# The expert layer's input moved to the bottom of the partitions, and the loads of scattered gates begun within the first layer

## The chip, the core and the metric

The kernel runs on one core of one Trainium2 chip. The metric is device time in microseconds (us) of one execution; lower is better. TensorE is called PE here, its weight loads PEld, VectorE DVE, ScalarE ACT, GpSimd POOL, and SyncE SP. SP does no arithmetic here: it issues most DMA transfers, one after the other, and an issue that waits holds back those behind it.

## The reference

A batch of 256 tokens of width 1024 goes through two transformer blocks in float32. The first block mixes by sliding-window attention and retention, with gated output, and has a SwiGLU layer. The second block mixes by spatial gating and banded attention with a learned bias over relative positions, and has a PEER expert layer, in which this change lies:

```python
def block(xb):                                   # 128 tokens at a time
    q = (xb @ w_query).reshape(128, 8, 2, 128)   # 8 heads, two half queries
    sc = jnp.einsum('thpd,hpkd->thpk', q, sub_keys)
    s_top, i_top = lax.top_k(sc, 16)
    ...                                          # 16 x 16 candidates of each head
    best, pos = lax.top_k(cand, 16)
    eidx = jnp.take_along_axis(cand_idx, pos, axis=-1)      # of 16384 experts
    g = jax.nn.softmax(best, axis=-1)
    u = jnp.take(expert_u, eidx, axis=0)
    h = jax.nn.gelu(jnp.einsum('thkd,td->thk', u, xb))
    vv = jnp.take(expert_v, eidx, axis=0)
    return jnp.einsum('thk,thkd->td', g * h, vv)
```

## The kernel before

**The expert layer is done densely.** Instead of gathering 128 experts for each token, the kernel computes all 16384 for all 256 tokens. The first layer (`first_layer(j)`, 128 steps) multiplies 128 experts' rows of `peer_u` with the input `xb` and puts the gelu into `S`, a tile of [128 experts, 128 steps j, 256 tokens] that holds every activation. The second layer (`second_layer`, 128 steps) multiplies `S[:, j]` with `peer_v`. In between, each entry of `S` is multiplied by its gate, which is zero for experts that were not chosen. All products are made of three matmuls with operands split in a high and a low part: `unit` (lines 77 to 100) loads a weight piece `raw` on SP's queue, ACT copies it to `whi` (line 95), and DVE makes `wlo` (line 96). There are four `raw` buffers and, in this layer, three pairs of `whi` and `wlo`. A step of the first layer is 24 matmuls of 256 columns into a bank named `mm`; a step of the second is 12 of 512 columns, into four banks `ax` that all 128 steps add to. Its left operands are the high and low part of `S[:, j]`, made by `split` (ACT line 154, DVE line 155), in tiles named `keys` (two buffers) and `q` (three).

**The gates come on two ways.** For tokens 0 to 127 (`TH` is 128) they are formed on the core: `form` and `combine` build them by matmuls of one-hot tiles during the first layer (PE line 940, names `A` and `G`) and multiply `S` by them; the tiles of this lie in a pool `comb`. `done` counts the tokens that are through. For tokens 128 to 255, POOL scatters the gates into a matrix `cmat` in HBM with indirect transfers that add (line 830). `gates(j)` (lines 1040 to 1047) loads four steps' worth, a tile `C` of [128, 4, 128], on POOL's queue and multiplies it into `S[:, j:j+4, 128:]` on DVE (line 1047).

**Memory sets the order.** SBUF pools are stacked from both ends of each partition. The pool `gates` that holds three `C` buffers takes the place of `comb`, so the kernel closes `comb` after the first layer's 128 steps and only then opens `gates`:

```python
        while done < TH:
            combine(128)
        groups.close()
        with tc.using_default_side("right"):
            gp = self.pool("gates", 1, groups)
```

The framework turns this into waits: whoever writes into a reused place waits for the last user of what lay there. `comb` also holds `gt`, the tile through which every pair of first-layer steps passes to the gates already in `S` (ACT line 1001, DVE line 1002), up to the last pair. The pool `xb` (the layer's input, 16 KB of each partition) lies on the right side too. Instructions are ordered on each engine by a scheduler that gives weight pieces a lead (`AHEAD`); `issue_after` ties a gate multiply to a place behind the latest `wlo`.

**Earlier users that the change touches.** In the first block, `aq`, `ak` and `avt` are queries, keys and values of the windowed attention, and `att` is its output. In the second block `rel` is the bias (1 MB in HBM), loaded by `load_const` (line 215) and partly overwritten by a POOL memset (line 543). `x3`, the residual input, is loaded at step 120 of the second layer into the place of `gates` (line 1077) and added to the result at the end (line 1083).

Of the kernel before, what the change touches and what calls it, by code (L numbers as in the profile page):

```python
# [7 lines left out]
F32 = mybir.dt.float32  # L8
F32R = mybir.dt.float32r
# [19 lines left out]
T = 256  # L29
TH = 128  # L30
# [13 lines left out]
class Net:  # L44
# [173 lines left out]
    def run(self):  # L218
        self.wpools, self.turn = [], 0
        with self.tc.using_default_side("right"):  # L220
            self.weights("wb", self.stack, 4, 3)
        with ExitStack() as st:
            self.res = self.pool("res", 2, st)
            self.work = self.pool("work", 2, st)
            actp = self.pool("actp", 2, st)
            with ExitStack() as sw:
                with self.tc.using_default_side("right"):
                    self.weights("wa", sw, 0, 3)
                x2, h, acc, acg = self.block1(actp)
                x3, h, acc = self.block2(actp, x2, h, acc, acg)  # L230
            self.wpools.pop()
            self.peer(st, x3, h, acc)

    def block1(self, actp):
        nc, a, tc = self.nc, self.a, self.tc
        mult, add, sub = OP.mult, OP.add, OP.subtract
        with ExitStack():
# [16 lines left out]
            both = self.const.tile([128, 192], F16, name="iota16")  # L254
# [4 lines left out]
            with ExitStack() as s1:  # L259
                p = self.pool("mix", 1, s1)  # L260
                p2 = self.pool("mix2", 2, s1)
                aq = p.tile([128, 4, T], F32, name="aq")
                ak = p.tile([128, T], F32, name="ak")
                avt = p.tile([128, T], F32, name="avt")
                av = p.tile([128, 2, 128], F32, name="av")
                rq = p.tile([128, 4, T], F32, name="rq")
                rk = p.tile([128, 4, T], F32, name="rk")
# [32 lines left out]
                                                self.ident)  # L300
                        nc.scalar.activation(av.rearrange("p a b -> p (a b)"), ps[:, :T], AF.Copy)

                att = self.new_acts(p, 4, "att", 1)
                probs = [self.att1_probs(p, tb, aq, ak, mask) for tb in range(2)]
                rv = p.tile([128, 2, D], F32, name="rv")
                room = p.tile([128, 8, 512], F32, tag="gate", name="room")
# [58 lines left out]
            with ExitStack() as s1:  # L365
                p = self.pool("ffn", 1, s1)
# [8 lines left out]
                for f in range(KF):  # L375
# [12 lines left out]
                    if 5 <= f < 21:  # L388
                        self.blanked.append(nc.sync.dma_start(out=blank[:, (f - 5) * 1024:(f - 4) * 1024],
                                                              in_=zero).ins)  # L390
                    if f == 1:
                        continue
                    for f0, (g, u) in enumerate(early, f + 1 - len(early)):
                        gu = p2.tile([128, 2, T], F32, name="gu")
                        if f0:
                            nc.vector.tensor_tensor(out=gu, in0=g, in1=R[:, None, :].to_broadcast([128, 2, T]),
                                                    op=mult)
# [129 lines left out]
    def block2(self, actp, x2, h, acc, acg):  # L527
        nc, a = self.nc, self.a
        mult, add, sub = OP.mult, OP.add, OP.subtract
        with ExitStack() as s1:  # L530
            p = self.pool("m2", 1, s1)
# [7 lines left out]
            r = self.tiny.tile([128, 2], F32, name="rd", bufs=1)  # L539
            self.rsqrt(r, ss, 2, 1.0 / D)  # L540
            nc.vector.tensor_tensor(out=r, in0=r, in1=r1, op=mult)
            bias = self.load_const(p, "rel", [128, 8, T])
            nc.gpsimd.memset(bias[0:64, :, 192:256], NEG)
            wsT = self.load_const(p, "wsT", [128, 8, 128])
            nc.gpsimd.memset(wsT[64:128, :, 0:64], 0.0)
# [169 lines left out]
    def peer(self, st, x3, h, acc):  # L715
        nc, a, tc = self.nc, self.a, self.tc
        mult, add, sub = OP.mult, OP.add, OP.subtract
        with tc.using_default_side("right"):
            xb = self.new_acts(self.pool("xb", 1), tag="xb", bufs=1)
            gs = self.pool("gs", 1).tile([128, 4, TH], F16, name="gs")  # L720
            qp = self.pool("query", 1)
            hold = self.pool("hold", 1)
            late = ExitStack()
            p = self.pool("topk", 1, late)
            pick = p.tile([128, 3, 128], F32, name="pick")
        hand = self.pool("hand", 2, st)
        x3t = tc.dram_tile([2, 128, D], F32, name="x3t")
        stop = p.tile([128, 4, 2, 2, 16], F32, name="stop")
# [31 lines left out]
        put_by = list(self.blanked)  # L760
        after = mybir.DependencyInfo(mybir.DependencyClass.Sync, mybir.DependencyReason.DATA)
# [135 lines left out]
        done = 0  # L897
        S, cp, ga = None, None, None

# [29 lines left out]
        def combine(jd):  # L929
            nonlocal done  # L930
            if made < TH:
                form()
            if len(formed) < 2 and made < TH:
                return
            t0 = done
            A, G = formed.pop(0)
            C = self.ax_bank()
            for t in range(4):
                for i in range(2):
                    nc.tensor.matmul(C[:, t * 128:t * 128 + 128], lhsT=A[:, t], rhs=G[i][:, t], start=i == 0,  # L940
                                     stop=i == 1)
            C = C.rearrange("p (t j) -> p j t", t=4)
            nc.vector.scalar_tensor_tensor(S[:, :jd, t0:t0 + 4], C[:, :jd], 1.0 / GSCALE, S[:, :jd, t0:t0 + 4],
                                           op0=mult, op1=mult)
            if jd < 128:
                nc.scalar.activation(S[:, jd:, t0:t0 + 4], C[:, jd:], AF.Copy, scale=1.0 / GSCALE)
            done += 4
# [41 lines left out]
        def first_layer(j):  # L989
            nonlocal pair  # L990
            e = j % 2
            if e == 0:
                pair = self.mm_bank()
            self.gemm_t(pair[:, e * T:e * T + T], a["peer_u"][j], xb, 8)
            if e == 0:
                return
            js = slice(j - 1, j + 1)
            p3 = pair.rearrange("p (e t) -> p e t", e=2)
            if done:
                gt = cp.tile([128, 2, TH], F32, name="gt", bufs=2)  # L1000
                nc.scalar.activation(gt[:, :, :done], p3[:, :, :done], AF.Gelu_apprx_tanh)
                nc.vector.tensor_tensor(out=S[:, js, :done], in0=S[:, js, :done], in1=gt[:, :, :done], op=mult)
            if done < T:
                nc.scalar.activation(S[:, js, done:], p3[:, :, done:], AF.Gelu_apprx_tanh)

# [2 lines left out]
            ready = pump(PQ)  # L1008
        st.close()
        S = self.pool("S", 1).tile([128, 128, T], F32, name="S")  # L1010
        c = RAWQ
        groups = ExitStack()
        for j in range(128):
            first_layer(j)
            if c < 16 and j % QE == QE - 1:
                query(c)
                c += 1
                pump(PQ)
            elif c == 16 and last:
                score(*last)  # L1020
                last = None
            if not ready:
                ready = pump(PU)
                if ready:
                    start = j
                    with tc.using_default_side("right"):
                        cp = self.pool("comb", 1, groups)
                    ga = cp.tile([128, TH], F32, name="ga")
                    nc.scalar.activation(ga, gs[:, 0], AF.Copy)
            elif j % 2:  # L1030
                while done < TH and (done + len(formed) * 4) * (GP - start) < TH * (j - start):
                    combine(j + 1)
        while done < TH:
            combine(128)
        groups.close()
        with tc.using_default_side("right"):
            gp = self.pool("gates", 1, groups)
        cview = self.cmat.rearrange("(a b t) o -> a b (t o)", a=128, b=128)

        def gates(j):  # L1040

            C = gp.tile([128, 4, 128], F32, name="C", bufs=3)
            i = nc.gpsimd.dma_start(out=C, in_=cview[:, j:j + 4]).ins
            for o in put_by:
                tc.add_manual_dep(i, o.name, after, reason="all heads have been added")
            with tc.issue_after(self.last_low):
                nc.vector.tensor_tensor(out=S[:, j:j + 4, TH:], in0=S[:, j:j + 4, TH:], in1=C, op=mult)

        gates(0)
        gates(4)  # L1050
        banks = [[self.ax_bank() for _ in range(2)] for _ in range(2)]

        def second_layer(j, tb, w, s, dhs):
# [8 lines left out]
        for j in range(128):  # L1062
            w = self.unit(a["peer_v"][j], 1024)
            s = [qp.tile([128, T], F32R, tag=t, name=t, bufs=n) for t, n in (("keys", 2), ("q", 3))]
            self.split(S[:, j], s[0], s[1])
            if j < 126:
                for tb in range(2):
                    second_layer(j, tb, w, s, ((0, 1),))
            else:
                held.append((j, w, s))  # L1070
            if j % 4 == 0 and j < 120:
                gates(j + 8)
            if j == 120:
                groups.close()
                with tc.using_default_side("right"):
                    x3 = self.pool("x3", 1).tile([128, 2, D], F32, name="x3")
                nc.sync.dma_start(out=x3, in_=x3t.rearrange("b t d -> t b d"))
# [94 lines left out]
```

## Time and profile before

| what | us |
|---|---|
| median of 3 runs (lowest, highest) | 1307.9 (1306.65, 1308.27) |
| the profiled execution: its time | 1307.3 |
| its span, first to last instruction | 1305.5 |
| PE busy with matmuls | 1285.2 (98%) |
| DVE busy | 906.7 (69%) |
| ACT busy | 719.9 (55%) |
| POOL busy | 262.9 (20%) |

The time of an execution is 1.8 us more than the span: what lies before the first and after the last instruction. PE's busy time counts the matmuls with their pipelined ends, so 98% does not say that it ran at its peak; the 20 us that are missing are waits. Times within the span are given from its start. The first layer of the experts runs from about 546 to 942 us, the second from 950 to 1301 us.

### The profile page before, as it was taken

Reading aid. Unit: us, or ns where it says so; the run is one execution under the profiler, and the core shown is the slowest. Engines: PE = TensorE matmul, PEld = TensorE weight load, DVE = VectorE, ACT = ScalarE, POOL = GpSimd, SP = SyncE. Lnnn points to the kernel's source line nnn. Section 1 sums busy time; section 2 is a strip of 40 time slices with the busy share of each in tenths; the row PEclk is TensorE's granted clock in tenths of the full one; section 3 lists DMA queues with packets and bytes.
Section 4 is the critical chain, followed back from the end, with each engine's and each line's share of the span. In section 5 each row is a group of like instructions: output and inputs, shape, how many; then the busy total and the mean of one; then the engine's idle time right before and its main releaser. Section 6 shows DMA issues by size and latency. Waiting matters only on the chain.

```text
span 1305.5 us, 23587 instructions
## 1 busy us (share of the span) xinstructions
PE 1285.2 (98%) x9125; PEld 1196.0 (92%) x9125; DVE 906.7 (69%) x1790; ACT 719.9 (55%) x1163; POOL 262.9 (20%) x173
## 2 busy tenths in 40 slices
PE   8999999999999999999999999999889999999998
PEld 7878999999999899999999999999878888888887
DVE  7767677766666877998885656665456666666665
ACT  5455545545454776554556666665445555555553
POOL 2000000000000000057778777740000000000000
PEclk9999999999999999999999999999989999999999
DMA  7645559966667535577777777765567777777764
GB/s 262 190 146 160 176 181 322 310 192 182 176 192 250 162 106 184 170 182 185 179 183 178 173 167 173 165 172 168 180 192 218 218 218 218 216 220 216 217 219 133
DMA packets 90928, 253.02 MB, mean 194 GB/s; under 512 B 26944, under 2 KB 28736, under 8 KB 90688
## 3 DMA queue, kind: packets, MB, share of 16 engines
q1 hardware_dynamic: 68816, 241.45, 59.9%
q0 software_dynamic: 20992, 8.46, 5.7%
q8 instruction: 71, 1.16, 0.4%
q10 hardware_dynamic: 1008, 1.61, 0.3%
q14 instruction: 41, 0.34, 0.1%
HBM read 240.93 MB, written 10.55 MB: 193 GB/s over the span
## 4 chain that ended last, share of the span: by engine, by line
PE 97%; DVE 2%; DMA 1%; issue 0%; ACT 0%; ACTq 0%; DVEq 0%
PE ax L1058 27%; PE mm L110 22%; PE mm L111 22%; PE mm L112 22%; PE ax L940 1%; PE ax L886 1%; DVE wlo L96 0%; DMA C<-cmat 0%; DMA small<-in_small_dram 0%; ACT whi L95 0%; PE ax L676 0%; PE ax L711 0%; PE ax L477 0%; PE ax L465 0%; PE ax L698 0%
## 5 line engine op out<-in xcount | busy, mean ns | idle before, releaser
L96 DVE TENSOR_TENSOR wlo<-raw,whi 128x1024 fp32r<-128x1024 f32 (+2 forms) x433 | 524.4, 1213 | 239.7 <-ACT whi L95 236.4
L95 ACT ACTIVATE whi<-raw 128x1024 fp32r<-128x1024 f32 (+3 forms) x439 | 457.6, 1045 | 315.3 <-PE mm L111 228.3
L110 PE MATMUL mm<-xbh,whi 128*128 128x256 f32 x1104 | 315.8, 286 | 0.0
L112 PE MATMUL mm<-xbh,wlo 128*128 128x256 f32 x1104 | 312.1, 283 | 0.9 <-DVE wlo L96 0.9
L111 PE MATMUL mm<-xbl,whi 128*128 128x256 f32 x1104 | 311.9, 283 | 0.0
L830 POOL DMA_INDIRECT cmat<-best,pos x128 | 235.1, 1837 | 215.9 <-DVE itop L739 153.7
L110 PE MATMUL mm<-acth,whi 128*128 128x256 f32 x848 | 239.0, 282 | 2.4 <-DVE aq L291 1.5
L111 PE MATMUL mm<-actl,whi 128*128 128x256 f32 x848 | 237.3, 280 | 2.4 <-DVE actl L252 2.4
L112 PE MATMUL mm<-acth,wlo 128*128 128x256 f32 x848 | 236.3, 279 | 0.0
L112 PEld LDWEIGHTS mm<-xbh,wlo 128*128 128x128 f32 x1104 | 211.4, 192 | 1.1 <-DVE wlo L96 1.1
L110 PEld LDWEIGHTS mm<-xbh,whi 128*128 128x128 f32 x1104 | 211.5, 192 | 0.1
L111 PEld LDWEIGHTS mm<-xbl,whi 128*128 128x128 f32 x1104 | 211.6, 192 | 0.0
L1058 PE MATMUL ax<-whi,keys 128*128 128x512 f32 x512 | 159.3, 392 | 8.0 <-ACT keys L154 8.0
L110 PEld LDWEIGHTS mm<-acth,whi 128*128 128x128 f32 x848 | 159.3, 188 | 3.6 <-DVE aq L291 1.7
L111 PEld LDWEIGHTS mm<-actl,whi 128*128 128x128 f32 x848 | 159.5, 188 | 3.1 <-DVE actl L252 3.0
L112 PEld LDWEIGHTS mm<-acth,wlo 128*128 128x128 f32 x848 | 159.4, 188 | 0.2 <-DVE wlo L96 0.2
L1058 PE MATMUL ax<-wlo,keys 128*128 128x512 f32 x512 | 158.9, 391 | 0.0
L1058 PE MATMUL ax<-whi,q 128*128 128x512 f32 x512 | 158.8, 391 | 0.0
L154 ACT ACTIVATE keys<-S 128x256 fp32r<-128x256 f32 x128 | 53.4, 418 | 161.4 <-PE ax L1058 155.4
L1058 PEld LDWEIGHTS ax<-whi,keys 128*128 128x128 f32 x512 | 96.8, 189 | 28.2 <-ACT keys L154 8.2
L1058 PEld LDWEIGHTS ax<-wlo,keys 128*128 128x128 f32 x512 | 96.8, 189 | 20.2
L1058 PEld LDWEIGHTS ax<-whi,q 128*128 128x128 f32 x512 | 96.7, 189 | 20.2
(284 smaller groups left out, 1409.8 us busy)
## 6 DMA issues: line engine op xcount, KB each, us to landing
raw<-in_peer_u_dram SPq DMA_DIRECT2D x128, 512.0 KB, 3.7
raw<-in_peer_v_dram SPq DMA_DIRECT2D x128, 512.0 KB, 4.3
raw<-in_w_in_b_dram SPq DMA_DIRECT2D x32, 512.0 KB, 4.2
raw<-in_w_in_a_dram SPq DMA_DIRECT2D x31, 512.0 KB, 4.2
raw<-in_w_gate_dram SPq DMA_DIRECT2D x22, 512.0 KB, 4.2
raw<-in_w_up_dram SPq DMA_DIRECT2D x22, 512.0 KB, 4.3
raw<-in_w_out_dram SPq DMA_DIRECT2D x16, 512.0 KB, 4.4
cmat<-zero SPq DMA_DIRECT2D x16, 512.0 KB, 7.3
```

Of the source, the lines that this page charges most:

```text
L95: self.last_copy = nc.scalar.activation(hi[:, s], raw[:, s], AF.Copy).ins
L96: low = (engine or nc.vector).tensor_tensor(out=lo[:, s], in0=raw[:, s], in1=hi[:, s].bitcast(F32), op=OP.subtract)
L110: mm(ps, lhsT=left[0], rhs=right[0], start=first, stop=False)
L111: mm(ps, lhsT=left[0], rhs=right[1], start=False, stop=False)
L112: mm(ps, lhsT=left[1], rhs=right[0], start=False, stop=last)
L154: nc.scalar.activation(hi, src, AF.Copy)
L830: i = nc.gpsimd.indirect_dma_start(self.cmat, bass.IndirectOffsetOnAxis(ap=ps[:, hd, 1, k:k + 1], axis=0), bs[:, hd, 1, k:k + 1], None, co ...
L886: nc.tensor.matmul(bank[:, tb, e], lhsT=qT[:, tb * 128:tb * 128 + 128], rhs=keys[:, e], start=True, stop=True)
L940: nc.tensor.matmul(C[:, t * 128:t * 128 + 128], lhsT=A[:, t], rhs=G[i][:, t], start=i == 0, stop=i == 1)
L1058: nc.tensor.matmul(banks[tb][d], lhsT=s[left][:, ts], rhs=w[right][:, d * 512:d * 512 + 512], start=first, stop=end)
```

## The change

It has two parts. First, `xb` goes from the right end to the bottom of the left side, into a pool `xbp` that stands there from the start. Since the place is there early, the attention's `aq`, `ak`, `avt` (as one tile `qkv`), then `rel`, use the half that is later the low part of `xb`, and `att` uses the half that is later its high part. The pool of activations `actp` follows directly above. `rel` is thus loaded into the place of `qkv`, no longer into a pool of the second block.

Second, `gt` gets a pool `gelu` of its own, and `comb` is closed as soon as the last tokens are combined, within the first layer. `gates` is opened there, and three `C` tiles are fetched. `fetch` and `apply` are what `gates(j)` was, taken apart. The first `apply` stands at step 121 of the first layer, the others four steps ahead of use (before: eight), each followed by the fetch for twelve steps ahead.

```diff
         with ExitStack() as st:
+            actp = self.pool("actp", 2, st)
             self.res = self.pool("res", 2, st)
             self.work = self.pool("work", 2, st)
-            actp = self.pool("actp", 2, st)
...
-                aq = p.tile([128, 4, T], F32, name="aq")
-                ak = p.tile([128, T], F32, name="ak")
-                avt = p.tile([128, T], F32, name="avt")
+                qkv = self.xbp.tile([128, 8, T], F32, tag="xbl", name="qkv", bufs=1)
+                aq, ak, avt = qkv[:, 0:4], qkv[:, 4], qkv[:, 5]
...
-                att = self.new_acts(p, 4, "att", 1)
+                both = self.xbp.tile([128, 8, T], F32R, tag="xbh", name="att", bufs=1)
+                att = both[:, 0:4], both[:, 4:8]
...
-            bias = self.load_const(p, "rel", [128, 8, T])
+            bias = self.xbp.tile([128, 8, T], F32, tag="xbl", name="rel", bufs=1)
+            nc.sync.dma_start(out=bias, in_=a["rel"])
...
-            xb = self.new_acts(self.pool("xb", 1), tag="xb", bufs=1)
...
+        xb = self.new_acts(self.xbp, tag="xb", bufs=1)
...
-                gt = cp.tile([128, 2, TH], F32, name="gt", bufs=2)
+                gt = gtp.tile([128, 2, TH], F32, name="gt")
...
+        def fetch(j):
+
+            C = gp.tile([128, 4, 128], F32, name="C", bufs=3)
+            i = nc.gpsimd.dma_start(out=C, in_=cview[:, j:j + 4]).ins
+            for o in put_by:
+                tc.add_manual_dep(i, o.name, after, reason="all heads have been added")
+            return C
+
+        def apply(j, C):
+            with tc.issue_after(self.last_low):
+                nc.vector.tensor_tensor(out=S[:, j:j + 4, TH:], in0=S[:, j:j + 4, TH:], in1=C, op=mult)
...
-            elif j % 2:
+            elif j % 2 and not fill:
                 while done < TH and (done + len(formed) * 4) * (GP - start) < TH * (j - start):
                     combine(j + 1)
-        while done < TH:
-            combine(128)
-        groups.close()
...
-        gates(0)
-        gates(4)
+                if done == TH:
+                    hots.close()
+                    with tc.using_default_side("right"):
+                        gp = self.pool("gates", 1, groups)
+                    fill = [fetch(4 * i) for i in range(3)]
+            if j == 121:
+                apply(0, fill.pop(0))
...
-            if j % 4 == 0 and j < 120:
-                gates(j + 8)
+            if j % 4 == 0 and j < 124:
+                apply(j + 4, fill.pop(0))
+                if j < 116:
+                    fill.append(fetch(j + 12))
```

Of the instructions, PE has the same in the same order. The other engines have the same ones too, some at another place. On DVE, at the passage from the first to the second layer, these rows stood before (`gt` is the first layer's gelu, `S<-S,C` a gate multiply, `q<-S,keys` the low part of a second-layer operand):

```order
L1002 TENSOR_TENSOR S<-S,gt 128x2x128
L1047 TENSOR_TENSOR S<-S,C 128x4x128 x2
L155 TENSOR_TENSOR q<-S,keys 128x256
L1047 TENSOR_TENSOR S<-S,C 128x4x128
L155 TENSOR_TENSOR q<-S,keys 128x256 x2
```

The first row is that of the last pair of steps. Now the first multiply and the low parts of steps 0 and 1 stand four pairs earlier, right behind the last combine (`S<-ax,S`):

```order
L945 SCALAR_TENSOR_TENSOR S<-ax,S 128x118x4
L96 TENSOR_TENSOR wlo<-raw,whi 128x1024
L1025 TENSOR_TENSOR S<-S,C 128x4x128
L96 TENSOR_TENSOR wlo<-raw,whi 128x1024
L1004 TENSOR_TENSOR S<-S,gt 128x2x128
L155 TENSOR_TENSOR q<-S,keys 128x256 x2
L96 TENSOR_TENSOR wlo<-raw,whi 128x1024 x2
```

The second multiply has moved ahead of the last pair, and the third follows behind the low part of step 3. On ACT, the high parts of steps 0, 1 and 2 stood together behind the last pair's gelu; now those of steps 0 and 1 stand behind the gelu of an earlier pair, with weight copies and four more pairs behind them:

```order
L1003 ACTIVATE gt<-mm 128x256
L1006 ACTIVATE S<-mm 128x2x128
L154 ACTIVATE keys<-S 128x256 x2
L95 ACTIVATE whi<-raw 128x1024 x2
```

On SP's queue the load of `rel` stood in the second block, ahead of `wsT`. Now it stands in the first, among the weights that follow the windowed attention's scores, ten pieces of `w_in_b` after that matrix began:

```order
L90 DMA raw_997<-in_w_in_b_dram 128x1024
L544 DMA rel_4880<-in_rel_dram 128x2048
L90 DMA raw_1015<-in_w_in_b_dram 128x1024
```

With it the memset of `rel` on POOL has moved ahead of the memset of `zero`. At the end of SP's queue, the load of `x3` has moved behind four more pieces of `peer_v`, since the last gate multiply comes four steps later.

## Rows read from the trace of the kernel before

**Rows 1.** The page, its head and part 1: busy time, share, instructions.

```profile
span 1305.5 us, 23587 instructions
PE 1285.2 (98%) x9125; PEld 1196.0 (92%) x9125; DVE 906.7 (69%) x1790; ACT 719.9 (55%) x1163; POOL 262.9 (20%) x173
```

**Rows 2.** Waits of PE: waiter, releaser; us in total, times, longest.

```profile
PE ax L1058 <- ACT keys L154: 8.0, 1, 8.0
```

**Rows 3.** Chain that ended last: start, length, what.

```profile
944.49 0.34 DVE S L1002
...
945.13 3.82 DMA C<-cmat
949.05 0.70 DVE S L1047
```

**Rows 4.** Timeline of PE between the layers: start, length, instruction.

```profile
941.86 0.28 PE L111 MATMUL mm<-xbl,whi 128*128 128x256 f32 x1
941.98 0.28 PE L112 MATMUL mm<-xbh,wlo 128*128 128x256 f32 x1
950.24 1.22 PE L1058 MATMUL ax<-whi,keys 128*128 128x512 f32 x2 [7.98 <-ACT keys L154]
...
956.35 0.63 PE L1058 MATMUL ax<-wlo,keys 128*128 128x512 f32 x2
...
958.65 0.62 PE L1058 MATMUL ax<-whi,keys 128*128 128x512 f32 x2
...
961.38 0.62 PE L1058 MATMUL ax<-whi,keys 128*128 128x512 f32 x2
```

**Rows 5.** Windows: length; PE, PEld, DVE, ACT, POOL busy (instructions), granted clock, DMA share, GB/s.

```profile
946.00:947.00 1.00, 0.00 (x0) 0.00 (x0) 0.00 (x0) 0.00 (x0) 0.84 (x2) 0.53 0.77 295
955.00:956.00 1.00, 1.00 (x4) 0.71 (x4) 0.43 (x1) 0.56 (x2) 0.00 (x0) 0.50 0.00 0
```

**Rows 6.** Timeline of PE: the last combine of tokens 0 to 127.

```profile
912.80 0.62 PE L940 MATMUL ax<-G,A 128*128 128x128 f16 x8
```

**Rows 7.** Tile C: its loads on POOL (ns min/median/max) and their landing.

```profile
L1043 POOL DMA_DIRECT2D C<-cmat x32: 536/536/599, 945.1 to 1234.1; - x32
DMA to landing us min/median/max: 2.9/4.1/4.7
```

**Rows 8.** Timeline of DVE behind the last combine, and at the first layer's end.

```profile
917.40 1.22 DVE L96 TENSOR_TENSOR wlo<-raw,whi 128x1024 fp32r<-128x1024 f32 x1 [1.32 <-ACT whi L95]
920.28 1.22 DVE L96 TENSOR_TENSOR wlo<-raw,whi 128x1024 fp32r<-128x1024 f32 x1 [1.66 <-ACT whi L95]
921.42 0.42 DVE L1002 TENSOR_TENSOR S<-S,gt 128x256 f32<-128x256 f32 x1
923.16 1.22 DVE L96 TENSOR_TENSOR wlo<-raw,whi 128x1024 fp32r<-128x1024 f32 x1 [1.32 <-ACT whi L95]
...
943.27 1.22 DVE L96 TENSOR_TENSOR wlo<-raw,whi 128x1024 fp32r<-128x1024 f32 x1 [1.65 <-ACT whi L95]
```

**Rows 9.** Timeline of ACT behind the last combine.

```profile
920.42 0.38 ACT L1004 ACTIVATE S<-mm 128x256 f32<-128x256 f32 x1
922.07 1.06 ACT L95 ACTIVATE whi<-raw 128x1024 fp32r<-128x1024 f32 x1 [1.28 <-issue]
```

**Rows 10.** Timeline of PE in the first block: the last scores.

```profile
56.08 1.92 PE L435 MATMUL ax<-ak,aq 64*128 64x256 f32 x8 [1.12 <-DVE s L441]
```

**Rows 11.** Timeline of SP there: issues from the eleventh piece of w_in_b on.

```profile
64.97 13.65 SPq L90 DMA_DIRECT2D raw<-in_w_in_b_dram  x6
```

**Rows 12.** Window between the two (columns as in rows 5).

```profile
58.00:65.00 7.00, 7.00 (x31) 5.67 (x31) 6.79 (x18) 5.48 (x20) 0.00 (x0) 1.00 0.03 13
```

**Rows 13.** Tile rel: us from issue to landing.

```profile
DMA to landing us min/median/max: 5.1/5.1/5.1
```

**Rows 14.** Timelines of SP and DVE at the end: x3's load and first use.

```profile
1266.52 0.38 SPq L1077 DMA_DIRECT2D x<-x3t  x1
1298.17 1.37 DVE L1083 TENSOR_TENSOR x<-ax,x 128x512 f32<-128x512 f32 x2 [1.62 <-PE ax L1058]
```

More of the change, by code (lines that the diff above doesn't have):

```diff
@@ L221, in run @@
             self.weights("wb", self.stack, 4, 3)
+        self.xbp = self.pool("xb", 1)
         with ExitStack() as st:
+            actp = self.pool("actp", 2, st)
             self.res = self.pool("res", 2, st)
             self.work = self.pool("work", 2, st)
-            actp = self.pool("actp", 2, st)
             with ExitStack() as sw:
@@ L1010, in peer @@
         S = self.pool("S", 1).tile([128, 128, T], F32, name="S")
+        cview = self.cmat.rearrange("(a b t) o -> a b (t o)", a=128, b=128)
+        def fetch(j):
[7 more added lines that the diff above has]
+                nc.vector.tensor_tensor(out=S[:, j:j + 4, TH:], in0=S[:, j:j + 4, TH:], in1=C, op=mult)
         c = RAWQ
-        groups = ExitStack()
+        groups, hots, fill = ExitStack(), ExitStack(), None
         for j in range(128):
@@ L1026, in peer @@
                     with tc.using_default_side("right"):
-                        cp = self.pool("comb", 1, groups)
+                        gtp = self.pool("gelu", 2, groups)
+                        cp = self.pool("comb", 1, hots)
                     ga = cp.tile([128, TH], F32, name="ga")
                     nc.scalar.activation(ga, gs[:, 0], AF.Copy)
-            elif j % 2:
+            elif j % 2 and not fill:
                 while done < TH and (done + len(formed) * 4) * (GP - start) < TH * (j - start):
                     combine(j + 1)
-        while done < TH:
-            combine(128)
-        groups.close()
[L1036 to L1047, printed above, removed]
-        gates(0)
-        gates(4)
+                if done == TH:
[5 more added lines that the diff above has]
+                apply(0, fill.pop(0))
         banks = [[self.ax_bank() for _ in range(2)] for _ in range(2)]
```

## The prediction

> **What bounds the kernel now.** I read the page first: PE is busy for 1285.2 of 1305.5 us, so nothing but PE's own waits (20.3 us in all) and its pace can give time back [rows 1]. The view of waits says where these lie: a single wait of 8.0 us, for ACT to make a second-layer operand, is the largest of them [rows 2]. The chain that ended last shows what stands behind that operand: the last pair of the first layer passes DVE at line 1002, then POOL's load of the first gates begins at 945.13, DVE uses it at 949.05, ACT follows, and PE starts again [rows 3]. PE's timeline gives both ends. In the first layer a matmul starts every 0.12 us, the last one at 941.98; the first of the second layer starts at 950.24 [rows 4]. The gap to where it would have started without a wait (942.10) is **8.14 us**.
>
> The reader should also see what comes after the gap. The window at 946 has a granted clock of 0.53, while PE stands still, and that at 955 has 0.50, the lower of the two levels (1.2 GHz in place of 2.4), while PE is busy throughout [rows 5]. From 950.24 to 956.35 PE does seven pairs of second-layer matmuls in 6.11 us; from 958.65 to 961.38 it does six pairs in 2.73, 0.455 each [rows 4]. Seven pairs at that pace are 3.185 us, so the low clock costs another **2.93 us**.
>
> **The change, part by part.**
>
> *The first gate load.* It now needs only the last use of `comb`, the combine's matmuls, which begin at 912.80 and end at 913.42 [rows 6]; `gt`, which kept `comb` to the last pair, has a place of its own. The scatters into `cmat` are over by then, and POOL has nothing else to do. Before, the releasing DVE instruction ended at 944.83, and DVE used the gates at 949.05: 4.22 us from release to use [rows 3]. The same distance from 913.42 puts the gates at 917.64; with the shortest and longest landing of the 32 loads in place of the first one's (2.9 and 4.7 against 3.82), at 916.7 to 918.5 [rows 3, 7].
>
> *What waits for it.* DVE's order puts the multiply behind the `wlo` that ends at 918.62 [rows 8]. So the gates are there when their turn comes, at either bound. The multiply takes 0.70 us [rows 3] and ends at about 919.3, before the next `wlo` at 920.28 [rows 8]. ACT's two `keys` follow its gelu, which ends at 920.80, and ACT is idle until 922.07: 1.27 us of room [rows 9]. One operand takes at most 0.49, the time from the end of DVE's multiply at 949.75 to PE's start [rows 3, 4]; two are 0.98. DVE's two `q` follow the gate product that ends at 921.84, with 1.3 us of room until 923.16 [rows 8]; they have its 256 columns, so I take its 0.42 us for each, 0.84 in all. I cost all of this at **nothing**: DVE and ACT idle over a microsecond before nearly every weight copy here. If the cover were gone it would cost the overrun alone, about 1 us.
>
> *How late it might be.* `wlo` at 920.28 comes some 1.2 us after its buffer came free (ACT's copy of 1.06 comes first) [rows 8, 9]. With three buffers, two steps of 24 matmuls at 0.12 us stand before its use [rows 4], so PE wants it near 919.1 + 5.76 = 924.9. It may start 3.4 us late (1.22 for itself), and the gates may arrive at about 923.0 without cost to PE: 5 us after the expected time.
>
> *The passage to the second layer.* PE then goes on at 942.10 with steps 0 and 1, whose operands have been made some 20 us earlier. Step 2's weights are the ones that come last: their `wlo` begins at 943.27 and ends at 944.49 [rows 8], and two steps of six pairs at 0.455 us make PE reach them at 942.10 + 5.46 = 947.6 [rows 4]. Three microseconds remain. The operand of step 2 waits for a `keys` buffer that step 0 frees at about 944.8; as in every later step it has one step, 2.73 us, to be made. No wait is added there, and without a standstill I see no reason for the clock to fall, so both amounts go: **8.14 + 2.93 = 11.07 us**.
>
> *The later gate multiplies.* There are still 32, and as many loads. They stand four steps ahead of use in place of eight, 10.9 us at 2.73 a step. Each load is issued when the multiply three groups before has freed its buffer, at least eight steps (21.8 us) before its own multiply; it lands in at most 4.7 [rows 7]. Cost nothing.
>
> *`rel` on SP's queue.* The load now waits for the last scores, which end at 58.00 [rows 10], and holds back the weights behind it. The next of these is issued at 64.97 anyway, since its buffer is not free earlier [rows 11], and in between the DMA engines are at 0.03 of their time [rows 12]. The load took 5.1 us [rows 13]: 58.0 + 5.1 = 63.1, before 64.97. Cost nothing; were the stretch not empty, it would be up to 5.1 us of delay for a weight piece, before the reserve of ready pieces. Its memset on POOL follows there, with `zero` behind it, which is not wanted before the feed-forward layer. Taking the load out of the second block gives nothing either, since no wait of PE there is near the size of the one above [rows 2].
>
> *`x3`.* Its load comes four pieces, 10.9 us, later against PE. Before, 31.6 us lay between it and its first use [rows 14]; 20.7 remain for 1 MB, for which `rel` shows 5.1 [rows 13]. Nothing. The shared tiles `qkv` and `att` only put other addresses under the same instructions. Nothing.
>
> **The sum.** The profiled execution took 1307.3; minus 11.07 that is 1296.2. The median of the runs is 0.6 above that execution, so I forecast **1296.8** for a median, 0.85% faster.
>
> **Rivals.**
>
> 1. *Part of it comes back.* Either a shorter wait takes the place of the long one (the weights of the second layer's first steps no longer get 8 us to run ahead), or the clock falls all the same. For it: with no standstill, three and more steps pass with only the 3 us of reserve counted above. Against: the whole second layer runs on the same reserves, and its matmuls have that one wait alone [rows 2]. With the clock's share lost, 1296.8 + 2.93 = 1299.7; with a wait up to half of the old one, 1300.9.
> 2. *It does not do what it says.* If some user of `comb`'s place other than the combine remains to the last pair, the load starts at 945 as before: 1307.9. Against: `gt` is the only tile of that pool in use after 913.4.
> 3. *Slower: the first gate multiply holds DVE and ACT.* Both take their instructions in order, and behind the multiply and the `keys` that wait for it stand the weights of the first layer. The price is the time by which the gates come after 923.0; it outweighs the gain once they come after 923.0 + 11.1 = 934.1, which is 20 us after the issue. Against: the longest of 32 landings is 4.7, and an issue on POOL took 536 to 599 ns, beside a busy DVE or an idle one [rows 7]. With an arrival at 940 it would be 1296.8 + 17.0 = 1313.8. The Trainium skill, DMA: Bandwidth & Descriptors, section SWDGE vs HWDGE vs iDMA, speaks for this one: descriptors of loads that GpSimd issues are written to SBUF, and DVE in its two-port mode locks GpSimd out of it. By that rule the loads, moved from a stretch where DVE waits into one where it works, would be issued later; the trace does not bear that out: the loads before, nearly all of them beside DVE's second-layer work, show no issue over 599 ns [rows 7].
>
> **How the numbers follow.** My forecast has a chance of 0.80, with a range of its own of 1295.0 to 1298.4 (the runs differ by 1.6 us among themselves, and the overruns above are about 1 us). Rival 1 has 0.13, rival 2 0.04, rival 3 0.03. A measurement here can tell about 0.2%, 2.6 us, from no change. Faster by more takes in the forecast and rival 1 (0.93), within that is rival 2 (0.04), slower is rival 3 (0.03). The range goes from 1295.0 to 1300.2: the forecast and most of rival 1.
>
> **What the profile after would show.** Right: POOL's first loads of `C` at about 913.7, in a stretch where PE is busy; line 1025's first multiply before 920; no wait of PE for `keys`; the first second-layer matmul within 0.3 us of the last of the first layer; a granted clock of 1.00 through the passage; `rel` issued near 58 and landed before 65; the span near 1294.4. Wrong: a wait of PE for `whi` or `wlo` between 920 and 950, a window at 0.50 near 945, a wait of DVE for `C` over a microsecond, or first-block weights landing later than before behind `rel`.

## The result, and the profile after

| | us, median (lowest, highest) |
|---|---|
| before, 4 runs | 1307.3 (1306.06, 1308.27) |
| after, 4 runs | 1288.0 (1287.51, 1289.34) |
| the profiled execution after: its time; its span | 1288.3; 1286.5 |

The change made the kernel faster by 1.5% (ratio 0.9854, 95% interval 0.9837 to 0.9872). The forecast was 1296.8 with a range of 1295.0 to 1300.2: the direction is right, the size is not. The time lies 7.0 us below the range.

The page of after, its head and part 1, answers to [rows 1]:

```profile
span 1286.5 us, 23584 instructions
PE 1276.2 (99%) x9125; PEld 1187.6 (92%) x9125; DVE 904.6 (70%) x1790; ACT 719.0 (56%) x1163; POOL 259.8 (20%) x173
```

PE has as many instructions as before, in the same order, and is busy for 9.0 us less. That is more than the low clock behind the gap could explain (2.93), and is the first sign that a matmul now takes less.

PE's timeline after, between the layers (start, length, instruction), answers to [rows 4]:

```profile
934.09 0.28 PE L112 MATMUL mm<-xbh,wlo 128*128 128x256 f32 x1
934.20 0.63 PE L1065 MATMUL ax<-whi,keys 128*128 128x512 f32 x2
...
936.94 0.62 PE L1065 MATMUL ax<-whi,keys 128*128 128x512 f32 x2
...
939.66 0.62 PE L1065 MATMUL ax<-whi,keys 128*128 128x512 f32 x2
```

The gap is gone: 0.11 us from the last matmul of the first layer to the first of the second. From here on six pairs take 2.74 us (934.20 to 936.94), the full pace, from the start. These rows and [rows 4] split the gain into three parts. The last matmul of the first layer starts at 934.09 in place of 941.98: 7.89 us are already won there. The first of the second layer starts at 934.20 in place of 950.24: 16.04, so the passage gives 8.15. The thirteenth pair of the second layer starts at 939.66 in place of 958.65: 18.99, so the clock gives another 2.95. The spans differ by 19.0. The sum of the prediction was 8.14 + 2.93. **Both of its terms came as they were worked out; what it lacks is the 7.89 us ahead of the passage.**

Windows after around the passage (length; busy time and instructions of PE, PEld, DVE, ACT, POOL; granted clock; DMA share; GB/s), against [rows 5]:

```profile
930.00:934.00 4.00, 4.00 (x37) 4.00 (x36) 3.17 (x4) 1.35 (x3) 0.54 (x1) 1.00 0.67 228
934.00:936.00 2.00, 2.00 (x12) 1.71 (x11) 0.62 (x1) 1.60 (x3) 0.00 (x0) 1.00 0.90 252
936.00:942.00 6.00, 6.00 (x28) 4.95 (x27) 4.06 (x6) 2.96 (x4) 0.00 (x0) 1.00 0.67 203
```

The granted clock stays at 1.00, the higher level, where PE goes on without a standstill.

All waits of PE after (waiter, releaser; total, times, longest), against [rows 2]:

```profile
PE mm L112 <- DVE wlo L96: 1.5, 1, 1.5
PE ax L436 <- DVE s L442: 1.1, 1, 1.1
PE ax L59 <- DVE ones L54: 1.1, 1, 1.1
PE mm L110 <- ACT acth L252: 1.0, 1, 1.0
PE mm L110 <- DVE qkv L291: 0.8, 1, 0.8
PE mm L111 <- DVE actl L253: 0.6, 2, 0.5
```

No wait for `keys` is left, and nothing took its place at the passage.

Where did the 7.89 us come from? I laid the starts of PE's 9125 matmuls of the two traces side by side, one by one. From 30 us to the first matmuls on `xb` they run together within 0.3 us. From there after gains steadily up to the passage, with one step back. Groups of PE by line and shape, first of before, then of after (count | busy, mean ns of one | idle before):

```profile
L110 PE MATMUL mm<-xbh,whi 128*128 128x256 f32 x1104 | 315.8, 286 | 0.0
L111 PE MATMUL mm<-xbl,whi 128*128 128x256 f32 x1104 | 311.9, 283 | 0.0
L110 PE MATMUL mm<-acth,whi 128*128 128x256 f32 x848 | 239.0, 282 | 2.4 <-DVE aq L291 1.5 <-ACT whi L95 0.5 <-ACT acth L251 0.4
L111 PE MATMUL mm<-actl,whi 128*128 128x256 f32 x848 | 237.3, 280 | 2.4 <-DVE actl L252 2.4
```

```profile
L110 PE MATMUL mm<-xbh,whi 128*128 128x256 f32 x1104 | 312.6, 283 | 0.0
L111 PE MATMUL mm<-xbl,whi 128*128 128x256 f32 x1104 | 308.2, 279 | 0.0
```

`xbh` and `xbl` are the high and low part of `xb`. One matmul on `xb` fell from 286 to 283 and from 283 to 279 ns. The last two rows of before are the same shapes on other moving operands, `acth` and `actl` (the high and low part of the blocks' activations): 282 and 280 ns, in the same trace. So the slower matmul was to be seen before the change. The mean hides the pace, since neighbours overlap; the distance of their starts (I call it the pitch) is 119.84 ns before and 117.02 after, over some 3200 neighbouring matmuls on `xb` with nothing between them; on `acth` and `actl` it was 117.2 before already. For the 3312 matmuls on `xb` (three times 1104) the difference makes 9.3 us. About 1.1 of these were given back at one place near 570 to 580 us, where DVE sorts beside its weight copies, `wlo` came late, and PE waited for it (the first row of the waits above).

### The profile page after: what moved, and what is told of

Read it like the earlier page. It is cut to its first block, busy times and chain, and to the rows that moved or that the text cites. A ratio compares the mean times of both kernels' runs of the same rounds, so it can differ in the third digit from the quotient of the medians.

```text
span 1286.5 us, 23584 instructions
## 1 busy us (share of the span) xinstructions
PE 1276.2 (99%) x9125; PEld 1187.6 (92%) x9125; DVE 904.6 (70%) x1790; ACT 719.0 (56%) x1163; POOL 259.8 (20%) x173
## 4 chain that ended last, share of the span: by engine, by line
PE 94%; DVE 3%; DMA 1%; issue 0%; POOL 0%; ACT 0%; SPq 0%; ACTq 0%; POOLq 0%; DVEq 0%
PE ax L1065 27%; PE mm L110 21%; PE mm L111 21%; PE mm L112 21%; DVE wlo L96 1%; PE ax L942 1%; DMA raw<-in_w_in_a_dram 1%; PE ax L888 0%; DMA xT<-in_xT_dram 0%; DVE itop L741 0%; PE ax L678 0%; PE ax L713 0%; PE ax L478 0%; PE ax L466 0%; PE ax L700 0%
## 5 line engine op out<-in xcount | busy, mean ns | idle before, releaser
L110 PE MATMUL mm<-xbh,whi 128*128 128x256 f32 x1104 | 312.6, 283 | 0.0
L112 PE MATMUL mm<-xbh,wlo 128*128 128x256 f32 x1104 | 308.0, 279 | 1.7 <-DVE wlo L96 1.5
L111 PE MATMUL mm<-xbl,whi 128*128 128x256 f32 x1104 | 308.2, 279 | 0.0
L832 POOL DMA_INDIRECT cmat<-best,pos x128 | 232.1, 1813 | 219.1 <-DVE itop L741 155.4
L112 PEld LDWEIGHTS mm<-xbh,wlo 128*128 128x128 f32 x1104 | 207.4, 188 | 2.3 <-DVE wlo L96 2.3
L110 PEld LDWEIGHTS mm<-xbh,whi 128*128 128x128 f32 x1104 | 207.5, 188 | 0.2
L111 PEld LDWEIGHTS mm<-xbl,whi 128*128 128x128 f32 x1104 | 207.6, 188 | 0.0
```

The source lines that it names most:

```text
L110: mm(ps, lhsT=left[0], rhs=right[0], start=first, stop=False)
L111: mm(ps, lhsT=left[0], rhs=right[1], start=False, stop=False)
L112: mm(ps, lhsT=left[1], rhs=right[0], start=False, stop=last)
L832: i = nc.gpsimd.indirect_dma_start(self.cmat, bass.IndirectOffsetOnAxis(ap=ps[:, hd, 1, k:k + 1], axis=0), bs[:, hd, 1, k:k + 1], None, co ...
```

## The experiments

**First, the two parts apart, and two theories of the pitch.** The four kernels below ran side by side with before, which took 1307.9. Both theories blame the address of `xb`. Addresses here and below are those at which the programs place their tiles; the traces do not show them. The right stack's tiles begin 32 bytes past a multiple of 64; at the bottom `xb` begins on a multiple of 64. **Theory A**: what counts is where the moving operand begins. **Theory B**: what counts is the end of the partition at which it lies, beside the weights or away from them.

*The second part alone.* After, with `xb`, the attention's tiles, `rel` and `actp` where they were before (the edit in part):

```diff
-        self.xbp = self.pool("xb", 1)
...
-        xb = self.new_acts(self.xbp, tag="xb", bufs=1)
+            xb = self.new_acts(self.pool("xb", 1), tag="xb", bufs=1)
...
```

> Only the second part: the gate loads begin within the first layer, xb stays at the right end where it was and qkv, att and rel have their own tiles. Both theories of the 8 us that the prediction lacks put them into the address of xb, so both expect here the two terms of the sum alone: stall 8.14 and low clock 2.93, 1307.3 less 11.1 is about 1296, and a pitch of the first layer's matmuls of 119.9 ns as before. If the earlier loads themselves quicken the first layer, the time is near 1288 and the pitch near 117 ns.

Measured: 1296.4 (ratio to before 0.992, 0.9903 to 0.9937), pitch 119.83 ns. This is the forecast, 1296.8, within its own spread: **the prediction had costed the second part rightly and given the first one no term.**

*The first part alone.* Before, with `xb` at the bottom, the earlier users in its tiles and `actp` above it (the edit in part):

```diff
+        self.xbp = self.pool("xb", 1)
...
-            xb = self.new_acts(self.pool("xb", 1), tag="xb", bufs=1)
+        xb = self.new_acts(self.xbp, tag="xb", bufs=1)
...
```

> Only the first part: xb at the bottom with qkv, att and rel in its two tiles, the gates as before. Both theories expect the pitch of the first layer at 116.8 ns, the PE wait of 8 us and the low clock behind it still there, and a gain of about 7.9 us: 1299 to 1300. If the place of xb has nothing to do with it, 1307.

Measured: 1299.4 (0.9938, 0.9921 to 0.9954), pitch 117.04. PE's timeline between the layers shows the old gap still there:

```profile
935.44 0.27 PE L112 MATMUL mm<-xbh,wlo 128*128 128x256 f32 x1
944.30 1.22 PE L1060 MATMUL ax<-whi,keys 128*128 128x512 f32 x2 [8.58 <-ACT keys L154]
```

The first part gives 8.5 us by the medians, the second 11.5; together 20.0, where after was 18.5 to 19.3 below before in two measurements. The parts add up, with at most one or two microseconds lost.

*`xb` at the bottom, 32 bytes off.* After, with 32 bytes put under `xb` and 32 above it:

```diff
+        nc.gpsimd.memset(self.pool("gap0", 1).tile([128, 8], F32, name="gap0"), 0.0)
         self.xbp = self.pool("xb", 1)
...
+            nc.gpsimd.memset(self.pool("gap1", 1, st).tile([128, 8], F32, name="gap1"), 0.0)
             actp = self.pool("actp", 2, st)
```

> After, with xb still at the bottom but 32 bytes higher (its tiles then begin 32 bytes past a multiple of 64, as they did at the right end), and everything above it only 64 bytes higher. Theory A (what counts is where the moving operand starts against multiples of 64 bytes): pitch 119.9 ns, time near 1296. Theory B (what counts is that the moving operand lies away from the weights, at the other end): pitch 116.8 ns, time 1288.

Measured: 1298.9 (0.9939, 0.9922 to 0.9956), pitch on `xb` 117.65. Neither theory said this. Of the 10.5 us that its trace loses against after's, 8.6 lie ahead of the expert layer: the pitch on `acth` and `actl`, which the two gaps had moved up by 64 bytes, rose from 117.11 to 119.95. By theory A that move could do nothing, since these tiles still began on a multiple of 64.

*`xb` at the right end, 32 bytes lower.* Before, with such gaps ahead of and behind `xb`:

```diff
+            nc.gpsimd.memset(self.pool("gap0", 1).tile([128, 8], F32, name="gap0"), 0.0)
             xb = self.new_acts(self.pool("xb", 1), tag="xb", bufs=1)
+            nc.gpsimd.memset(self.pool("gap1", 1).tile([128, 8], F32, name="gap1"), 0.0)
```

> Before, with xb still at the right end but 32 bytes lower, so that its tiles begin on a multiple of 64 bytes; all that lies beyond it keeps its distance to such a multiple. Theory A (start against multiples of 64 bytes): pitch 116.8 ns, time 1299 to 1300, the stall and the low clock unchanged. Theory B (which end it lies at): pitch 119.9 ns, time 1307.

Measured: 1306.2, not to be told from before (0.9992, 0.9983 to 1.0002), which looks like theory B, but the trace says otherwise: the pitch on `xb` is 118.29, between the two, and PE had gained 4.3 us by the end of the first layer. It then lost some 3.3 in the second, whose pitch rose from 226.67 to 228.89 ns: the gaps had moved `keys` and `q`, its stationary operands, by 64 bytes. **Both theories as stated fell.** The stationary operand counts too, and a multiple of 64 is not what matters.

**Second, the matmul by itself.** Now theory A became: the pitch follows from the distance of the two operands' start addresses modulo some length. Two kernels hold nothing but matmuls and the loading of their operands; `sta` and `mov` are tiles that begin at given distances from a multiple of 1024 bytes:

```python
        def group(m, s):
            nonlocal n
            for k in range(REPS):
                g = slice(k % 8 * 128, k % 8 * 128 + 128)
                nc.tensor.matmul(banks[n % 4][:, :COLS], lhsT=sta[s][:, g], rhs=mov[m][:, :COLS],
                                 start=k == 0, stop=k == REPS - 1)
            n += 1
```

> The matmul alone: the expert layer is left out and the output is zeros and products of loaded numbers. 136 groups of 48 matmuls of 256 columns run back to back on TensorE with no other engine busy; mN is a moving operand that starts N bytes past a multiple of 1024, sN a stationary one. Theory A, as the four runs before leave it (the pitch follows from the phases of the two operands, whichever end they lie at): with the weights at s224 the pitch is that of the kernel at the same phases, about 117.0 ns at m000 and m256, 117.6 at m288, 118.3 at m448, 119.9 at m480 and 119.9 at m320. Theory B (the end at which xb lies, or what other engines do to the memory there): all groups at one pitch, about 117, since all lie together and nothing else runs.

> As m1, with 512 columns and groups of 24. Theory A: m480 on s224 about 226.7 ns (the second layer of before and after), m480 on s160 about 228.9 (the second layer with keys and q 64 bytes lower), m480 on s000 about 233.3 and on s064 about 234.2 (the products of the second block). Theory B: one pitch for all groups.

Each ran once, with 112 groups (the expectation says 136), the first eight of them to warm up. Their pitches, from the starts of the matmuls behind a group's first few, by the moving operand's address minus the stationary one's, modulo 256 bytes (I call this the relative phase):

```
relative phase       0      32      64      96     128     160     192     224
256 columns, ns   120.0   117.8   117.8   119.8   118.7   118.6   117.8   118.3
                                                          117.3   113.3
512 columns, ns   226.8   233.3   229.1   233.4   233.3   234.3   233.3   233.3
```

Every start of the moving operand from 0 to 992 in steps of 32 was tried against one stationary one, and the values come back every 256. Moving both operands by the same amount changes nothing (0 against 0 to 224 against 224: 119.9 to 120.0). With no other engine at work and all tiles side by side, the pitches of the kernels are here again, within 0.2 ns: 119.84 at relative phase 0, 117.65 at 64, 118.29 at 224, 119.95 at 96, and of 512 columns 226.67 at 0, 228.89 at 64, 233.3 at 224 and 234.2 at 160. Only after's 117.0 at relative phase 32 is 0.8 lower than here. Theory B fell. At relative phases 160 and 192 some groups of 256 columns ran at a second, faster pitch throughout (at 192, two groups of twelve); that was not expected.

**Third, back in the kernel.** If the relative phase is all, `xb` must be fast at the right end and slow at the bottom once its phase is set so. Weights begin at 224 modulo 256 in all kernels so far. The next four kernels ran side by side with before, which took 1307.0.

```diff
+            nc.gpsimd.memset(self.pool("gap0", 1).tile([128, 56], F32, name="gap0"), 0.0)
             xb = self.new_acts(self.pool("xb", 1), tag="xb", bufs=1)
+            nc.gpsimd.memset(self.pool("gap1", 1).tile([128, 8], F32, name="gap1"), 0.0)
```

> Before, with xb still at the right end but 224 bytes lower, so that its tiles begin on a multiple of 256 bytes, and 32 bytes behind it, so that all that follows is 256 bytes lower. Theory A, now as the relative phase of the moving and the stationary operand modulo 256 bytes (here 32, as in after): pitch 117.0 ns, the wait and the low clock unchanged, time 1299 to 1300, as with xb at the bottom. Theory B (the end at which xb lies): 119.8 ns and 1307.

Measured: 1299.8 (0.9944, 0.9928 to 0.9959), pitch 116.99. At the right end, with 256 bytes of gaps as the only edit to before, `xb` is as fast as at the bottom.

```diff
+        nc.gpsimd.memset(self.pool("gap0", 1).tile([128, 56], F32, name="gap0"), 0.0)
         self.xbp = self.pool("xb", 1)
...
+        nc.gpsimd.memset(self.pool("gap1", 1).tile([128, 8], F32, name="gap1"), 0.0)
```

> After, with xb still at the bottom but 224 bytes higher, in the phase of the weights (relative phase 0), and 32 bytes above it, so that everything above is 256 bytes higher. Theory A: pitch 119.8 ns in the first layer of the experts, 117.1 in the blocks before it, time near 1296, which is what the prediction forecast. Theory B: 117.0 ns and 1288.

Measured: 1296.0 (0.9913, 0.9898 to 0.9928), pitch 119.84; that of `acth` and `actl` 116.94 (before: 117.2). Groups of PE in this kernel:

```profile
L110 PE MATMUL mm<-xbh,whi 128*128 128x256 f32 x1104 | 315.7, 286 | 0.0
L111 PE MATMUL mm<-xbl,whi 128*128 128x256 f32 x1104 | 311.9, 283 | 0.0
```

At the bottom, in the weights' phase, `xb` costs 286 and 283 ns again, as before the change, and the time is the one that was forecast. This settles the first part: its gain comes with the relative phase at either end of the partition, and the end itself has no share in it that these runs could tell.

**Fourth, another phase for the weights.** By the map above the products of 512 columns (weights moving, activations stationary) would gain at relative phase 64, and those of 256 columns lose nothing at 192. One gap of 160 bytes at the start of the right stack sets both:

```diff
         with self.tc.using_default_side("right"):
+            self.nc.gpsimd.memset(self.pool("gap0", 1).tile([128, 40], F32, name="gap0"), 0.0)
             self.weights("wb", self.stack, 4, 3)
```

> After, with the whole right stack 160 bytes lower, so that weights begin at phase 64. By the map of the two runs of the matmul alone: 256 columns at relative phase 192 in place of 32, both 117.8 there, so no change; the second layer stays at relative phase 0; the 384 products of 512 columns with weights as the moving operand go from relative phase 224 (233.3 ns) to 64 (229.1 ns), 1.6 us in all: time near 1286.4. If the order of high and low parts in the kernel makes relative phase 192 worth 117.8 ns where 32 is worth 117.0 there, some 6500 matmuls lose 0.8 ns each, 5 us: 1291 to 1292.

> The changed kernel once more, on the same chip as the three others, to compare them with: 1288.0.

Measured: 1269.7 (ratio to before 0.9715, 0.9702 to 0.9729) against 1288.5 for after beside it (0.986, 0.9845 to 0.9875). **The gap alone is worth 18.8 us, about as much as the whole change; this is the fastest version.** The products of 512 columns went to 229.04 ns as expected, worth 1.6 us. The rest was not expected: the pitch on `xb` fell from 117.04 to 114.73 in the mean, on `acth` and `actl` from 117.12 to 114.31, and in long stretches to 113.4. By these pitches `xb` gives 7.7 us of the gain, `acth` and `actl` 7.3, `hid` (the feed-forward layer's activations, 117.78 to 113.33 on 528 matmuls) 2.3 and the 512 columns 1.6. PE's timeline, first of after, then of this kernel:

```profile
932.80 0.28 PE L110 MATMUL mm<-xbh,whi 128*128 128x256 f32 x1
...
933.85 0.28 PE L110 MATMUL mm<-xbh,whi 128*128 128x256 f32 x1
```

```profile
914.13 0.28 PE L110 MATMUL mm<-xbh,whi 128*128 128x256 f32 x1
...
915.15 0.28 PE L110 MATMUL mm<-xbh,whi 128*128 128x256 f32 x1
```

Each pair of rows is nine matmuls apart: 1.05 us, 117 ns each, and 1.02 us, 113 ns each. The low pitch is that of the second value at relative phase 192 in the map. Both values of the map are in this trace: up to 684 us the steps of 24 matmuls on `xb` run now at 117.8 (39 steps by their last 16 starts, as at 600 us), now at 113.3, and behind that all run at 113.3.

**Fifth, which of the two pitches a stretch gets.** Matmuls alone again, run once, with weights and moving parts in the kernel's order. A `step` is 24 matmuls, as in the first layer, and a group two steps at one relative phase `d`, with `r` short matmuls ahead:

```python
        for r in range(8):
            for d in mov:
                for i in range(r):
                    nc.tensor.matmul(banks[n % 4][:, 256:384], lhsT=sta[0][:, :128], rhs=mov[0][0][:, :128],
                                     start=True, stop=True)
                for _ in range(2):
                    step(d)
```

> The matmul alone again, the expert layer left out: groups of 48 matmuls of 256 columns in the kernel's order of high and low parts, eight for each relative phase (0, 32, ... 224), each behind 0 to 7 short matmuls of 128 columns that change how a group is entered. In the run of the matmul alone, relative phase 192 ran at 117.8 ns in ten groups of 12 and at 113.3 in two, and in the kernel with weights at phase 64 long stretches ran at 113.4. If one relative phase has two steady paces and the entry chooses: relative phase 192 shows both within these eight groups, each holding through its group, and 0 shows 120.0 alone. If the order of high and low parts makes the lower pace: all eight groups at 192 near 113.4. If only the work of other engines in the kernel brings it: all eight at 117.8.

The pitch of the eight groups of each relative phase (how many groups ran at it):

```
  0: 120.0 (8)               128: 118.7 (6), 120.0 (2)
 32: 116.7 (5), 117.8 (3)    160: 118.8 (5), 117.4 (3)
 64: 117.8 (7), 113.3 (1)    192: 113.3 (7), 117.8 (1)
 96: 120.0 (8)               224: 118.4 (8)
```

PE's timeline in this kernel, two groups at relative phase 192, the first without short matmuls ahead, the second behind one (rows of the low part alone, one in three matmuls):

```profile
86.32 0.28 PE L135 MATMUL b<-l,w 128*128 128x256 f32 x1
...
90.21 0.28 PE L135 MATMUL b<-l,w 128*128 128x256 f32 x1
...
132.15 0.28 PE L135 MATMUL b<-l,w 128*128 128x256 f32 x1
...
135.88 0.28 PE L135 MATMUL b<-l,w 128*128 128x256 f32 x1
```

Both stretches are 33 matmuls: 3.89 us, 117.9 ns each, and 3.73 us, 113.0 ns each. The operands, the shape and the granted clock (1.00) are the same; only what ran ahead differs, and a group keeps its pitch to its end. So some relative phases have one steady pitch and some have two, with no other engine at work, and how a stretch is entered seems to have a part in which it gets. The order of high and low parts does not settle it: at 192 the seven groups behind short matmuls took the low pitch and the one without them the high one. Nor does the program alone: on `xb` after has both of relative phase 32's values (101 steps of 24 matmuls at 116.7 ns and 35 at 117.8; its 117.0 is their mean), and another execution of the same kernel, `after_again`, gave the other value to 18 of these steps, all of them before 600 us. What decides is not shown.

## Why the prediction was wrong, by its own steps

- **The step that failed** is the sentence that the shared tiles "only put other addresses under the same instructions. Nothing." and with it the silence about `xb` itself: the move to the bottom got no term in the sum. It moved `xb` from relative phase 0 to 32 against the weights, which is worth 2.8 ns on each of 3312 matmuls, 9.3 us, of which 7.9 were left at the passage. The trace of before held the evidence: same shape, same line, 286 ns on `xbh` and 282 on `acth`, 119.84 against 117.2 ns from start to start. The prediction took the first layer's 0.12 us a matmul as it stood [rows 4] and never compared it with the others. No rival had a faster matmul either, so the range ended at 1295.0.
- **The standstill and the low clock**: 8.15 and 2.95, predicted 8.14 and 2.93 [rows 4, 5]. The second part alone gave 1296.4, predicted 1296.8. So the mechanism that the prediction described is right, and it was not luck that its terms came out.
- **The first gate load** started right behind the last combine, and DVE's multiply directly behind a `wlo`, as forecast. Timelines of PE, POOL and DVE after, in this order:

```profile
905.68 0.62 PE L942 MATMUL ax<-G,A 128*128 128x128 f16 x8
```

```profile
906.89 0.60 POOL L1018 DMA_DIRECT2D C<-cmat  x1 [43.44 <-ACT whi L95]
```

```profile
910.23 1.23 DVE L96 TENSOR_TENSOR wlo<-raw,whi 128x1024 fp32r<-128x1024 f32 x1 [1.26 <-ACT whi L95]
911.51 0.69 DVE L1025 TENSOR_TENSOR S<-S,C 128x512 f32<-128x512 f32 x1
```

  The combine ends at 906.30. The multiply starts 5.2 us later and does not wait for `C`; predicted were 4.2 us to the gates, and a `wlo` that ends after that (913.42, 917.64 and 918.62 in the slower first layer of before). With the second part alone the first layer keeps that slower pace, and there the times themselves can be compared: loads from 913.8, forecast 913.7, and the multiply at 918.5, forecast 918.62. Tile `C` in that kernel:

```profile
L1016 POOL DMA_DIRECT2D C<-cmat x32: 536/536/599, 913.8 to 1233.6; - x32
L1023 DVE TENSOR_TENSOR S<-S,C x32: 682/683/693, 918.5 to 1265.3; 128x512 f32<-128x512 f32 x32
```

  In both kernels the load begins 0.6 us after the combine's last matmul. The view names ACT's `whi` as what ended POOL's wait; that it was the combine rests on these times.
- **The rivals.** Rival 1 found nothing coming back: the clock stays at 1.00 and no wait stands at the passage. Rival 2 fell with the load at 906.89. For rival 3, DVE did not wait for the gates, and issues on POOL beside DVE's work took no longer than before [rows 7]; the tile's loads after:

```profile
L1018 POOL DMA_DIRECT2D C<-cmat x32: 536/536/599, 906.9 to 1226.0; - x32
```

  The 5 us by which the gates might come late without cost were not tried: with a later load the scheduler moves the multiply too.
- **`rel`** was issued at 58.06, as forecast (58.0). It landed later than the estimate of 63.1: POOL's memset, which waits for it, starts at 64.8. That is still ahead of the next weight issue at 65.00, so it cost nothing. Tile `rel`, and SP's timeline, after:

```profile
L545 POOL MEMSET rel<- x1: 521/521/521, 64.8 to 64.8; 64x512 f32 x1
```

```profile
58.06 0.33 SPq L544 DMA_DIRECT2D rel<-in_rel_dram  x1
65.00 2.67 SPq L90 DMA_DIRECT2D raw<-in_w_in_b_dram  x2
```

## What to carry to other kernels

Where TensorE bounds a kernel, measure the distance between starts of matmuls of one shape, operand by operand, before costing a move of a tile at nothing: where equal shapes differ, the addresses may be the reason. The distance of moving and stationary operand modulo 256 bytes is a free parameter, set by a gap of some bytes in a memory stack, and here one such gap was worth 18.8 us, more than removing an 8 us standstill (11.5 with the low clock behind it). A gap moves everything stacked behind it, so look at all matmuls when you try one: a run whose time could not be told from before's hid a gain of 4.3 us and a loss of 3.3.

## What was not expected of the hardware

- The pitch of back-to-back matmuls depends on the relative phase of their operands: 113.3 to 120.0 ns for 256 columns of these operands, 226.7 to 234.3 for 512. The best phase for the one shape is among the worst for the other: 0 gives 226.8 for 512 columns and 120.0 for 256, the slowest there.
- At some relative phases there are two steady pitches (113.3 or 117.8 ns at 192), kept for a whole group of 48 matmuls. What ran ahead seems to have a part in the choice, but two executions of one kernel did not choose alike everywhere. What decides is open, and so is what repeats every 256 bytes. The runs show the rule, not its mechanism.
